# Where one of seven weight sums is made: on GpSimd from loaded tiles, or by accumulating transfers

## The chip, the cores and the metric

The kernel runs on one core of a Trainium2 chip. The metric is the device time of one execution in microseconds (us), the median of several runs. A separate profiled execution gives the trace. The engines are called here as in the profile: PE (TensorE, matrix products), DVE (VectorE), ACT (ScalarE), POOL (GpSimd) and SP (SyncE, which issues most loads).

## What is computed

A trunk of two layers, 256 tokens of width 1024, all in fp32. Each layer has two gated feed-forward blocks (FFN) around a mixer and a cross attention. What matters here is the first FFN of the first layer:

```python
def swiglu(h, w_gate, w_up, w_down):
    return (jax.nn.silu(h @ w_gate) * (h @ w_up)) @ w_down

h = x
for i in range(DEPTH):
    h = h + 0.5 * swiglu(rmsnorm(h, ffn1_norm[i]), ffn1_w_gate[i], ffn1_w_up[i], ffn1_w_down[i])
    ...            # mixer, cross attention
    h = h + 0.5 * swiglu(rmsnorm(h, ffn2_norm[i]), ffn2_w_gate[i], ffn2_w_up[i], ffn2_w_down[i])
```

`w_gate` and `w_up` are 1024 x 2816, `w_down` is 2816 x 1024.

## The kernel before

**Products in two halves.** Every fp32 weight tile is split before PE uses it: ACT writes its rounded copy `whi` (line 224), then DVE writes the rest `wlo` = w - `whi` (line 225, `Gran.split`). Each product is then three products on PE (lines 262 to 264, `mm3`): with `whi`, with `wlo`, and with `whi` against the low half of the activations. A piece of weights that is split at once is a "gran" of 128x1024; PE takes 12 products for a gran of the plain kind, 6 for one of the sets below. The tiles for `whi` and `wlo` rotate through four buffers, so splitting runs a few grans ahead of PE and no further.

**The sets of seven products.** Within an FFN, `ffn_hidden` (line 782) computes the hidden columns in chunks of 512. Some chunks get their gate and up columns together by a scheme with seven products in place of eight (`seven`, line 361). The weights of a set are four tiles of 512 x 512: b11 and b21, the upper and lower half of the up columns, b12 and b22, those of the gate columns. Three further operands are sums, described by the class `Sum` (line 180): x2 = x1 + b22 (with x1 = b11 + b12), x4 = x2 + b21 and x3 = b12 + b22. x1 goes to a tile of its own; x2 and x4 are made in place in x1's tile, x3 in place in b12's tile. The order of the products within a set is b11, x1, x2, b22, x3, b21, x4 (the tuple in line 887), each of two grans; between them `share` puts grans of other products, so that PE always has work.

**Who makes the sums.** x1 and x2 are one DVE addition of 128x2048 each (line 203). x3 and x4 are made by two transfers each: POOL issues them (line 199), and they add 512 KB from HBM onto what lies in the tile. `x2.load()` and `x3.load()` are called after the product with x1, `x4.load()` after the product with x2 (line 389). An engine's instructions run in the order in which they stand in its queue; the waits between engines are semaphores that the framework sets from the tiles read and written.

**The first part.** The first FFN (`norm is first_norm`) has three such sets, for the chunks c = 2, 3 and 4. The other three FFNs have four sets each. The first part's sets lie at about 45 to 82, 85 to 127 and 128 to 165 us of the trace.

Of the kernel before, what the change touches and what calls it, by code (L numbers as in the profile page):

```python
# [12 lines left out]
ALU = mybir.AluOpType  # L13
# [44 lines left out]
def trunk(ctx, tc, a, out):  # L58
    nc = tc.nc
# [15 lines left out]
    def acc(name):  # L75
        return pacc.tile([P, 512], F32, name=name, tag="acc")
# [4 lines left out]
    def work(name, n=512, dt=F32):  # L81

        return wk.tile([P, n], dt, name=name, tag="v", bufs=6) if n <= 256 else wk.tile([P, n], dt, name=name, tag="w")
# [24 lines left out]
    class Pipe:  # L108
# [4 lines left out]
        def after(self, us, f):  # L113
            self.q.append((self.t + us, f))
# [30 lines left out]
    class W:  # L145
# [6 lines left out]
        def load(self, k=None, nk=None):  # L152
            if k is None:
                if self.t is not None:
                    return
                k, nk = 0, self.nk
            if self.t is None:
                t = wp.tile([P, 2048], F32, name="w", tag="w")
                self.t = t[:, :self.nk * self.n].rearrange("p (k c) -> p k c", c=self.n)
            r0 = (self.k0 + k) * P  # L160
            nc.sync.dma_start(self.t[:, k:k + nk, :], self.src[r0:r0 + nk * P, self.c0:self.c0 + self.n]
                              .rearrange("(k p) c -> p k c", p=P))
# [17 lines left out]
    class Sum:  # L180
# [5 lines left out]
        def load(self):  # L186
            if self.t is not None:
                return
            self.l.load()
            if self.into is None:  # L190
                self.r.load()
                self.t = wp.tile([P, 2048], F32, name="w", tag="w").rearrange("p (k c) -> p k c", c=512)
            else:
                self.t = self.l.t
            w = self.r
            if self.into == "dma":
                for k in (0, 2):
                    r0 = (w.k0 + k) * P
                    nc.gpsimd.dma_start(self.t[:, k:k + 2, :], w.src[r0:r0 + 2 * P, w.c0:w.c0 + w.n]  # L199
                                        .rearrange("(k p) c -> p k c", p=P), accum_op=ALU.add)  # L200
            else:
                w.load()
                nc.vector.tensor_tensor(self.t, self.l.t, w.t, op=ALU.add)  # L203

    class Gran:

# [54 lines left out]
    def mm3(o, lh, ll, rh, rl, start, stop, onto=False):  # L261
        nc.tensor.matmul(o, lhsT=lh, rhs=rh, start=start, stop=False, skip_group_check=onto)  # L262
        nc.tensor.matmul(o, lhsT=lh, rhs=rl, start=False, stop=False, skip_group_check=onto)  # L263
        nc.tensor.matmul(o, lhsT=ll, rhs=rh, start=False, stop=stop, skip_group_check=onto)  # L264
# [93 lines left out]

    ONTO = {2: 0, 4: 0, 3: 1, 5: 1, 6: 1}

    def seven(b1, b2, x, mix, after, order=(0, 1, 2, 3, 5, 4, 6), second="dma"):

        b11, b21 = (W(b1[0], k, 4, b1[1], 512) for k in (0, 4))
        b12, b22 = (W(b2[0], k, 4, b2[1], 512) for k in (0, 4))
        x1 = Sum(b11, b12)
        x2 = Sum(x1, b22, second)
        x4 = Sum(x2, b21, "dma")
        x3 = Sum(b12, b22, "dma")
        banks = {}

        def a(t, h):
            return lambda k: tuple(v[:, t * P:(t + 1) * P] for v in pipe.need(x, 4 * h + k))

        def s(i):
            return lambda k: tuple(v[:, k * P:(k + 1) * P] for v in pipe.need(mix, i))
        plan = [(x1, s(0)), (b11, a(0, 0)), (b22, s(1)), (x2, s(2)), (b21, a(0, 1)), (x3, s(3)), (x4, a(1, 1))]
        out = []
        for i in order:
            w, lhs = plan[i]
            for k0 in (0, 2):  # L380
                def step(g, i=i, lhs=lhs, k0=k0):
                    if not k0:
                        banks[i] = banks[ONTO[i]] if i in ONTO else acc("seven")
                    for k in range(k0, k0 + 2):
                        lh, ll = lhs(k)
                        mm3(banks[i], lh, ll, g.hi[:, k - k0, :], g.lo[:, k - k0, :], k == 0 and i < 2, k == 3, onto=i in ONTO)
                        pipe.pe(0.68)
                    if k0:
                        for w in {0: (x2, x3), 3: (x4,)}.get(i, ()):
                            w.load()  # L390
                        after(i, banks)
                out.append((Gran(w.k0 + k0, 2, (w, 0, 512)), step))
        return out

    def share(hosts, s, counts):
        out, hosts = [], list(hosts)
        for i, n in enumerate(counts):
            out += hosts[:n] + s[2 * i:2 * i + 2]
            hosts = hosts[n:]
        return out + hosts  # L400
# [235 lines left out]
    first_norm = nrm = Norm(cols0, mixes=True)  # L636
# [145 lines left out]
    def ffn_hidden(nm, l, norm, fin, tail, extra=None):  # L782
# [31 lines left out]
        def extras(c):  # L814
            for i in (2 * c, 2 * c + 1):
                if extra and i in extra:
                    extra[i]()

        def seven_fin(c):
            us, t = {}, {}  # L820

            def after(i, b):
                v = nc.vector

                def copy():
                    t[i] = work(f"p{i}")
                    nc.scalar.copy(t[i], b[i])

                def c12():
                    us[0] = t[3]  # L830
                    v.tensor_tensor(us[0], b[2], t[3], op=ALU.subtract)
                    nc.scalar.copy(b[2], t[1])
                    nc.scalar.activation(us[0], us[0], AF.Silu, scale=norm.col[:, 0:1])

                def c22():
                    us[1] = t[0]
                    v.tensor_tensor(t[0], t[0], b[5], op=ALU.subtract)
                    nc.scalar.activation(t[0], t[0], AF.Silu, scale=norm.col[:, 1:2])
                    if c == 4:
                        extras(6)  # L840

                def up(r):
                    v.scalar_tensor_tensor(us[r], b[i], norm.col[:, r:r + 1], us[r], op0=ALU.mult, op1=ALU.mult)
                    if r:
                        pipe.after(T["hid"], lambda: turn(c, [us[0], us[1]], 512))
                        extras(c)
                pipe.after(0.7, {0: copy, 1: copy, 3: copy, 2: c12, 5: c22, 4: lambda: up(0), 6: lambda: up(1)}[i])
            return after

        def turn(c, us, n):  # L850
            for i in range(0, n // P, 2):
                tp = v2(small_ps("htp"))
                for j in range(2):
                    for t in range(2):
                        nc.tensor.transpose(tp[:, j, t * P:(t + 1) * P], us[t][:, (i + j) * P:(i + j + 1) * P], ident)  # L855
                hi = v2(slot("hid_hi", F32R))
                lo = v2(slot("hid_lo", F32R))
                nc.scalar.copy(hi, tp)
                nc.vector.tensor_tensor(lo, tp, hi.bitcast(F32), op=ALU.subtract)
                for j in range(2):  # L860
                    hid[4 * c + i + j] = (hi[:, j, :], lo[:, j, :])
        wg, wu = a[nm + "_w_gate"][l], a[nm + "_w_up"][l]
        wide([(wg, 0, 512)], norm, "gate", gate_fin(0), **({} if units else dict(single=True, eng=nc.gpsimd)))
        c = HID // 512
# [19 lines left out]
            n += d0[i:j] + d1[i:j]  # L884
        steps = []
        for c, k in counts.items():
            s = seven((wu, c * 512), (wg, c * 512), norm.x, norm.s, seven_fin(c), (1, 0, 3, 2, 5, 4, 6), "dve")
            steps += share(n[:sum(k)], s, k)
            n = n[sum(k):]
        assert not n  # L890
# [3 lines left out]
    def ffn(nm, l, norm, nxt, extra=None):  # L894
        fin = upd(0.5, nxt)
        ffn_hidden(nm, l, norm, fin, lambda hid, wd: down(wd, 1, [(12, 4), (16, 4)], hid, [], 12, fin), extra)
# [218 lines left out]
    def cross_attention(l, norm, kv, nxt):  # L1115
# [86 lines left out]
        wkv = a["xa_w_kv"][l]  # L1202
        q = [g for c in (2, 0) for g in columns(a["xa_w_q"][l], c * 256, norm, "xq", [q_fin(c), q_fin(c + 1)])]
        weave(share(q, seven((wkv, 1024), (wkv, 1536), kv.x, kv.s, mv_fin()), [2, 1, 1, 2, 1, 1, 0]))
        out_b(a["xa_w_o"][l], KT, ot, upd(1.0, nxt), (4, 0))

# [329 lines left out]
    def last(norm):  # L1536
# [71 lines left out]
        def tail(hid_, wd):  # L1608
            hid.append(hid_)
            gr.extend(Gran(k, 2, (w, 0, 512)) for w in [W(wd, k, 4, 512, 512) for k in (12, 16)] for k in (w.k0, w.k0 + 2))  # L1610
            return [(gr[0], run)]
        ffn_hidden("ffn2", 1, norm, first_half, tail, {12: final_gain})
        units.append((gr[1:], run))

# [72 lines left out]
```

## Time and profile before

| | |
|---|---|
| median of three runs | 1257.75 us (1257.62 to 1258.05) |
| profiled execution, its own time | 1258.38 us |
| its span in the trace | 1256.6 us |
| PE busy | 1247.1 us, 99% |
| DVE busy | 1057.2 us, 84% |
| ACT busy | 873.5 us, 70% |
| POOL busy | 162.5 us, 13% |
| granted PE clock, mean | 0.999 |

The trace lists each instruction with its start and length in us, its engine, its line in the kernel and the tiles it writes and reads. A number in square brackets behind an instruction is the time for which its engine stood idle just before, and what ended that idle time. A line such as `x3` at the end says that three like instructions in a row are shown as one, with their time from the first start to the last end. Instructions on DVE overlap a little: the next one starts some 0.07 us before the end that is listed for the one before.

### The profile page before, as it was taken

What the parts mean: (1) busy time and instruction counts of PE and PEld (TensorE: products, weight loads), DVE (VectorE), ACT (ScalarE), POOL (GpSimd) and SP (SyncE); (2) the same over time, 40 slices, a digit from 0 to 9 for tenths busy, and PEclk for the clock granted to TensorE, in tenths of its full rate; (3) what the DMA queues carried; (4) which work ended last, traced back from release to release, by engine and by line L of the source; (5) the groups of instructions that cost most, each with busy time, mean ns of one, the idle gap of its engine ahead of it and who ended that gap; (6) DMA issues with size and microseconds to landing.
All of it is one profiled execution on the core that took longest, in us unless ns stands there. A gap on an engine that the chain in (4) does not pass through costs nothing.

```text
span 1256.6 us, 18186 instructions
## 1 busy us (share of the span) xinstructions
PE 1247.1 (99%) x6751; PEld 1071.7 (85%) x6751; DVE 1057.2 (84%) x1451; ACT 873.5 (70%) x1388; POOL 162.5 (13%) x139
## 2 busy tenths in 40 slices
PE   9999999999999999999999999999999999999997
PEld 7888888788998888888888889999998898888886
DVE  6998787887787999887998976798898887898886
ACT  6676764686676776767776756777876775877772
POOL 1101102101101111110111000022233100011100
PEclk9999999999999999999999999999999999999999
DMA  9989976445776688987879977665636586489961
GB/s 330 301 255 259 314 256 208 137 165 170 222 214 170 165 252 260 293 246 234 240 198 268 311 247 221 192 193 168 201 134 185 169 246 182 157 251 256 258 190 34
DMA packets 161195, 275.03 MB, mean 219 GB/s; under 512 B 7209, under 2 KB 43730, under 8 KB 161106
## 3 DMA queue, kind: packets, MB, share of 16 engines
q1 hardware_dynamic: 137744, 229.75, 53.4%
q0 software_dynamic: 19744, 38.28, 17.7%
q10 hardware_dynamic: 3618, 5.84, 1.4%
q8 instruction: 53, 0.87, 0.3%
q14 instruction: 36, 0.29, 0.1%
HBM read 271.72 MB, written 2.13 MB: 218 GB/s over the span
## 4 chain that ended last, share of the span: by engine, by line
PE 94%; DMA 2%; DVE 2%; ACT 2%; issue 1%; POOLq 0%; POOL 0%; SPq 0%; ACTq 0%; DVEq 0%
PE out L262 9%; PE out L264 9%; PE out L263 9%; PE seven L263 8%; PE seven L262 8%; PE seven L264 8%; PE htp L855 1%; PE up L263 1%; PE up L264 1%; PE up L262 1%; PE xs L264 1%; PE xs L262 1%; PE xq L263 1%; PE xq L264 1%; PE xs L263 1%; PE xq L262 1%
## 5 line engine op out<-in xcount | busy, mean ns | idle before, releaser
L225 DVE TENSOR_TENSOR wlo<-w,whi 128x1024 fp32r<-128x1024 f32 (+2 forms) x532 | 639.4, 1220 | 134.6 <-ACT whi L224 126.8
L224 ACT CAST whi<-w 128x1024 fp32r<-128x1024 f32 (+2 forms) x534 | 551.0, 1039 | 245.2 <-PE out L264 84.0
L262 PE MATMUL out<-whi,hid_hi 128*128 128x512 f32 x336 | 132.3, 394 | 0.0
L264 PE MATMUL out<-whi,hid_lo 128*128 128x512 f32 x336 | 131.0, 390 | 0.0
L263 PE MATMUL out<-wlo,hid_hi 128*128 128x512 f32 x336 | 130.8, 389 | 0.0
L263 PE MATMUL seven<-wlo,s_hi 128*128 128x512 f32 x272 | 106.0, 390 | 0.6 <-DVE wlo L225 0.6
L262 PE MATMUL seven<-whi,s_hi 128*128 128x512 f32 x272 | 106.2, 390 | 0.0
L264 PE MATMUL seven<-whi,s_lo 128*128 128x512 f32 x272 | 105.9, 389 | 0.0
L199 POOL DMA_DIRECT2D w<-in_ffn_w_up_dram x30 | 36.7, 1268 | 346.6 <-DVE wlo L225 339.5
L203 DVE TENSOR_TENSOR w<-w 128x2048 f32<-128x2048 f32 x32 | 73.2, 2287 | 2.0 <-DMA w<-in_ffn_w_gate_dram 1.5
L264 PEld LDWEIGHTS out<-whi,hid_lo 128*128 128x128 f32 x336 | 63.1, 188 | 13.4
L263 PEld LDWEIGHTS out<-wlo,hid_hi 128*128 128x128 f32 x336 | 63.1, 188 | 12.6
L262 PEld LDWEIGHTS out<-whi,hid_hi 128*128 128x128 f32 x336 | 63.1, 188 | 12.5
L262 PE MATMUL seven<-whi,xh 128*128 128x512 f32 x180 | 70.5, 392 | 0.0
L264 PE MATMUL seven<-whi,xl 128*128 128x512 f32 x180 | 70.1, 389 | 0.0
L263 PE MATMUL seven<-wlo,xh 128*128 128x512 f32 x180 | 70.0, 389 | 0.0
L263 PEld LDWEIGHTS seven<-wlo,s_hi 128*128 128x128 f32 x272 | 51.1, 188 | 11.4 <-DVE wlo L225 1.0
L264 PEld LDWEIGHTS seven<-whi,s_lo 128*128 128x128 f32 x272 | 51.1, 188 | 10.7
L262 PEld LDWEIGHTS seven<-whi,s_hi 128*128 128x128 f32 x272 | 51.1, 188 | 10.4
L199 POOL DMA_DIRECT2D w<-in_ffn_w_gate_dram x30 | 36.9, 1467 | 176.2 <-DVE xst L1146 62.3
L264 PEld LDWEIGHTS seven<-whi,xl 128*128 128x128 f32 x180 | 33.8, 188 | 7.1
L262 PEld LDWEIGHTS seven<-whi,xh 128*128 128x128 f32 x180 | 33.8, 188 | 6.8
(395 smaller groups left out, 3013.7 us busy)
## 6 DMA issues: line engine op xcount, KB each, us to landing
w<-in_ffn_w_up_dram SPq DMA_DIRECT2D x40, 1024.0 KB, 7.8
w<-in_ffn_w_down_dram SPq DMA_DIRECT2D x40, 1024.0 KB, 9.3
w<-in_ffn_w_gate_dram SPq DMA_DIRECT2D x38, 1024.0 KB, 8.9
w<-in_ssd_w_in_dram SPq DMA_DIRECT2D x24, 1024.0 KB, 5.4
w<-in_xa_w_kv_dram SPq DMA_DIRECT2D x16, 1024.0 KB, 6.4
w<-in_ffn_w_gate_dram POOLq DMA_DIRECT2D x30, 512.0 KB, 9.7
w<-in_ffn_w_up_dram POOLq DMA_DIRECT2D x30, 512.0 KB, 7.2
w<-in_da_w_in_dram SPq DMA_DIRECT2D x12, 1024.0 KB, 5.2
```

The lines of the kernel that those rows point to most:

```text
L199: nc.gpsimd.dma_start(self.t[:, k:k + 2, :], w.src[r0:r0 + 2 * P, w.c0:w.c0 + w.n] .rearrange("(k p) c -> p k c", p=P), accum_op=ALU.add)
L203: nc.vector.tensor_tensor(self.t, self.l.t, w.t, op=ALU.add)
L224: nc.scalar.copy(hv, src)
L225: self.eng.tensor_tensor(self.lo[:, :, o:o + n], src, hv.bitcast(F32), op=ALU.subtract)
L262: nc.tensor.matmul(o, lhsT=lh, rhs=rh, start=start, stop=False, skip_group_check=onto)
L263: nc.tensor.matmul(o, lhsT=lh, rhs=rl, start=False, stop=False, skip_group_check=onto)
L264: nc.tensor.matmul(o, lhsT=ll, rhs=rh, start=False, stop=stop, skip_group_check=onto)
L855: nc.tensor.transpose(tp[:, j, t * P:(t + 1) * P], us[t][:, (i + j) * P:(i + j + 1) * P], ident)
```

## The change

For the three sets of the first part, x3 is no longer made by the two accumulating transfers. `seven` gets an argument `third`; where it is `"pool"`, `Sum.load` makes sure that b22 is loaded and lets POOL add it to b12's tile in four steps of 128x512. b22 is loaded anyway for its own product and for x2. All other sums, and the sets of the other FFNs, stay as they were.

```diff
@@ class Sum, load
             else:
                 w.load()
-                nc.vector.tensor_tensor(self.t, self.l.t, w.t, op=ALU.add)
+                if self.into != "pool":
+                    nc.vector.tensor_tensor(self.t, self.l.t, w.t, op=ALU.add)
+                    return
+                for k in range(4):
+                    nc.gpsimd.tensor_tensor(self.t[:, k, :], self.t[:, k, :], w.t[:, k, :], op=ALU.add)
@@ seven
-    def seven(b1, b2, x, mix, after, order=(0, 1, 2, 3, 5, 4, 6), second="dma"):
+    def seven(b1, b2, x, mix, after, order=(0, 1, 2, 3, 5, 4, 6), second="dma", third="dma"):
...
-        x3 = Sum(b12, b22, "dma")
+        x3 = Sum(b12, b22, third)
@@ ffn_hidden
-            s = seven((wu, c * 512), (wg, c * 512), norm.x, norm.s, seven_fin(c), (1, 0, 3, 2, 5, 4, 6), "dve")
+            s = seven((wu, c * 512), (wg, c * 512), norm.x, norm.s, seven_fin(c), (1, 0, 3, 2, 5, 4, 6), "dve",
+                      "pool" if norm is first_norm else "dma")
```

POOL's queue before, for the first two sets. In the first set w_584 is b12's tile, which becomes x3, and w_586 is x1's tile, which becomes x2 and then x4; in the second these are w_882 and w_884.

```order
L199 DMA w_584<-in_ffn1_w_gate_dram 128x2x512 [waits DMAHW1_49,DVE_49]
L199 DMA w_584<-in_ffn1_w_gate_dram 128x2x512
L199 DMA w_586<-in_ffn1_w_up_dram 128x2x512 [waits DMAHW4_49,DMAHW0_49,DMAHW5_49,DVE_49,Pool_49]
L199 DMA w_586<-in_ffn1_w_up_dram 128x2x512 [waits DVE_49]
L199 DMA w_882<-in_ffn1_w_gate_dram 128x2x512 [waits DMAHW1_49,DMAHW2_49,DVE_49,DMAHW3_49,Activation_49,Pool_49]
L199 DMA w_882<-in_ffn1_w_gate_dram 128x2x512
```

The same place in the queue with the change, where w_629 is b22's tile of the first set, and w_884 and w_975 are b12's and b22's of the second.

```order
L207 TENSOR_TENSOR w_584<-w_584,w_629 128x512 [waits DMAHW3_49,DMAHW1_49,DVE_49]
L207 TENSOR_TENSOR w_584<-w_584,w_629 128x512 x3
L199 DMA w_586<-in_ffn1_w_up_dram 128x2x512 [waits DMAHW4_49,DMAHW0_49,DMAHW5_49,DVE_49,Pool_49]
L199 DMA w_586<-in_ffn1_w_up_dram 128x2x512 [waits DVE_49]
L207 TENSOR_TENSOR w_884<-w_884,w_975 128x512 [waits DMAHW1_49,DMAHW2_49,DVE_49,DMAHW3_49,Activation_49,Pool_49]
L207 TENSOR_TENSOR w_884<-w_884,w_975 128x512 x3
```

Each pair of transfers has become four additions in the same place, and the first of them waits in the first set for one more load, that of b22.

DVE's queue with the change, from the sum x1 of the first set (w_586 from w_522, which is b11, and w_584) over the splits of x1's two grans and one other gran to the sum x2 and the splits behind it.

```order
L204 TENSOR_TENSOR w_586<-w_522,w_584 128x2048
L863 TENSOR_TENSOR hid_lo_576<-htp_570,hid_hi_575 128x512
L229 TENSOR_TENSOR wlo_583<-w_586,whi_582 128x1024
L229 TENSOR_TENSOR wlo_597<-w_586,whi_596 128x1024
L229 TENSOR_TENSOR wlo_615<-w_616,whi_614 128x1024
L204 TENSOR_TENSOR w_586<-w_586,w_629 128x2048
L229 TENSOR_TENSOR wlo_628<-w_586,whi_627 128x1024
```

Nothing has moved here: the queues of DVE, PE, ACT and SP hold the same instructions in the same order as before, under line numbers that are one to five higher.

## Rows read from the trace of the kernel before

**Rows 1.** The page's head: span, then each engine's busy time, share, instructions.

```profile
span 1256.6 us, 18186 instructions
...
PE 1247.1 (99%) x6751; PEld 1071.7 (85%) x6751; DVE 1057.2 (84%) x1451; ACT 873.5 (70%) x1388; POOL 162.5 (13%) x139
```

**Rows 2.** Waits of PE: us in total, times, longest.

```profile
PE seven L263 <- DVE wlo L225: 0.6, 1, 0.6
```

**Rows 3.** Timeline of PE, first set: start us, us, instruction, idle time before.

```profile
57.93 0.50 PE L263 MATMUL seven<-wlo,s_hi 128*128 128x512 f32 x1 [0.63 <-DVE wlo L225]
...
68.72 0.39 PE L262 MATMUL seven<-whi,s_hi 128*128 128x512 f32 x1
```

**Rows 4.** Timeline of DVE, first set.

```profile
48.42 0.68 DVE L859 TENSOR_TENSOR hid_lo<-htp,hid_hi 128x512 fp32r<-128x512 f32 x1
49.68 3.60 DVE L225 TENSOR_TENSOR wlo<-w,whi 128x1024 fp32r<-128x1024 f32 x3 [0.58 <-ACT whi L224]
53.20 2.28 DVE L203 TENSOR_TENSOR w<-w 128x2048 f32<-128x2048 f32 x1
56.66 6.90 DVE L225 TENSOR_TENSOR wlo<-w,whi 128x1024 fp32r<-128x1024 f32 x6 [1.17 <-ACT whi L224]
```

**Rows 5.** Busy us of PE, PEld, DVE, ACT, POOL in one stretch, set 2.

```profile
83.40:98.00 14.60, 14.60 (x74) 12.22 (x74) 14.60 (x16) 9.53 (x14) 0.80 (x1) 1.00 0.79 239
```

**Rows 6.** Timeline of POOL, first set and the attention behind it.

```profile
48.82 2.61 POOL L199 DMA_DIRECT2D w<-in_ffn_w_gate_dram  x2 [27.51 <-DVE w L203]
58.42 2.42 POOL L199 DMA_DIRECT2D w<-in_ffn_w_up_dram  x2 [6.99 <-issue]
...
202.36 1.29 POOL L930 TENSOR_TENSOR rt<-rt,rt 128x512 f32<-128x512 f32 x1 [9.90 <-DVE rt L929]
...
244.87 3.53 POOL L930 TENSOR_TENSOR rt<-rt,rt 128x512 f32<-128x512 f32 x2 [12.35 <-DVE rt L929]
```

**Rows 7.** Loads issued at 24 to 29, 69, 110 us: KB, us to landing; SP timeline.

```profile
w<-in_ffn_w_gate_dram SPq DMA_DIRECT2D x2, 1024.0 KB, 15.0
...
69.26 0.37 SPq L161 DMA_DIRECT2D w<-in_ffn_w_gate_dram  x1
w<-in_ffn_w_gate_dram SPq DMA_DIRECT2D x1, 1024.0 KB, 8.3
...
109.80 0.37 SPq L161 DMA_DIRECT2D w<-in_ffn_w_gate_dram  x1
w<-in_ffn_w_gate_dram SPq DMA_DIRECT2D x1, 1024.0 KB, 5.5
```

**Rows 8.** Timeline of DVE: one operation without POOL, three around POOL's adds.

```profile
93.42 1.21 DVE L225 TENSOR_TENSOR wlo<-w,whi 128x1024 fp32r<-128x1024 f32 x1
...
244.28 0.41 DVE L929 TENSOR_TENSOR rt<-k,cossinr 128x256 f32<-128x256 f32 x1
...
245.54 0.41 DVE L929 TENSOR_TENSOR rt<-k,cossinr 128x256 f32<-128x256 f32 x1
...
247.18 2.30 DVE L225 TENSOR_TENSOR wlo<-w,whi 128x1024 fp32r<-128x1024 f32 x1
```

**Rows 9.** Timeline of DVE, second set.

```profile
78.84 0.74 DVE L843 SCALAR_TENSOR_TENSOR p<-seven,rcol,p 128x512 f32<-128x512 f32 x1
...
80.89 2.58 DVE L225 TENSOR_TENSOR wlo<-w,whi 128x1024 fp32r<-128x1024 f32 x2 [0.18 <-ACT whi L224]
```

**Rows 10.** Timeline of PE: first use of two `wlo`, second and third set.

```profile
95.25 0.39 PE L263 MATMUL out<-wlo,hid_hi 128*128 128x512 f32 x1
...
125.16 0.39 PE L263 MATMUL out<-wlo,hid_hi 128*128 128x512 f32 x1
```

**Rows 11.** Timeline of DVE, third set.

```profile
117.27 0.68 DVE L837 TENSOR_TENSOR p<-p,seven 128x512 f32<-128x512 f32 x1
...
119.68 2.36 DVE L225 TENSOR_TENSOR wlo<-w,whi 128x1024 fp32r<-128x1024 f32 x2 [0.59 <-ACT whi L224]
...
122.62 3.48 DVE L225 TENSOR_TENSOR wlo<-w,whi 128x1024 fp32r<-128x1024 f32 x3
```

## The prediction

> **What bounds the kernel now.** I read the page's head first: TensorE (PE) is busy for 1247.1 us of a span of 1256.6 us [rows 1]. So nearly nothing can be won by freeing another engine, and whatever makes PE wait is added to the time in full. The waits of PE come next: apart from its start, the only one of note is 0.6 us, once, in the very stretch that the change touches, and it is a wait for VectorE's (DVE's) subtraction `wlo` [rows 2]. In the order of time this is the product with x2 of the first set: PE stands until 57.93 us, because the low half of the first half of x2 is ready only then [rows 3]. Then I read DVE around it [rows 4]: after the sum x1 come a `hid_lo` at 48.42, three `wlo` from 49.68, the sum x2 at 53.20, and from 56.66 the `wlo` that PE waits for. So in the first set a chain on DVE has no slack at all. In the second set DVE has no idle time either: it is busy for all 14.60 us from 83.40 to 98.00 [rows 5].
>
> The transfers are no bound that PE feels: in this first part no wait of PE leads to one.
>
> **What is removed.** Per set, two accumulating transfers of 512 KB by GpSimd (POOL), whose issue takes 2.61 us of POOL [rows 6], an engine that is idle for most of the time; nobody waits for these transfers in the trace. The other loads may land earlier without them. What that can be worth is bounded by what PE loses today in this stretch, 0.63 us [rows 3]; a loss there is no reason for. I take 0, since the wait of 0.63 us is for DVE and not for a load.
>
> **What is added.** Per set, four adds on POOL of 128x512, both inputs and the output in SBUF. The trace has the same operation elsewhere: 1.29 us alone [rows 6]. Four are 5.16 us. Behind them in the POOL queue are the transfers for x4, which go out at 58.42 in the first set, 9.6 us after the others [rows 6], and wait for splits of x2; even with every add doubled by waiting (10.3 us) they would hardly be held up. The product with x3 starts at 68.72 [rows 3], some 10 us after that, so the wait for x3 itself costs nothing.
>
> **When the adds start.** They wait for the sum x1 (DVE reads b12, which POOL overwrites) and for b22, which must now have landed. In the first set b22 is asked for before 29 us and lands 15.0 us after [rows 7], before the sum x1 ends. So the adds start where the transfers started, released by that sum, at 48.82 [rows 6]. In the second set b22 is asked for at 69.26 and lands after 8.3, at 77.6; in the third at 109.80 and after 5.5, at 115.3 [rows 7].
>
> **What an add costs DVE.** This is the term that decides. At 244.87 two adds stand ready on POOL while DVE has four `wlo` in a row; each `wlo` reads two inputs from SBUF, as the adds do. The two adds take 3.53 us instead of 2.6 [rows 6], and the `wlo` at 247.18 takes 2.30 us instead of the 1.21 of the one at 93.42 [rows 8]. So the two engines take turns: a whole add goes in between two `wlo`, and DVE stands still for 1.09 us. The DVE operation at 245.54, which reads one of its inputs from PSUM, takes 0.41 us during an add, as its like at 244.28 does before it [rows 8]: it isn't touched. The price is thus 1.09 us for each add that meets `wlo` work or a sum, and nothing beside a PSUM operation or an idle DVE. Its bounds are 0 and 1.29, the whole length of an add.
>
> The Trainium skill (SBUF — State Buffer, section "Who interferes with whom") says that a VectorE instruction with two SBUF inputs and a GpSimd instruction that reads SBUF exclude each other for the whole instruction, and that the loser waits outright. It speaks against this change; with the whole 1.29 us in place of the 1.09 us of the row, the sum below would be 9.8 us. The trace agrees that one waits outright, yet shows the smaller 1.09.
>
> **Set 1.** Four adds, 4 x 1.09 = 4.36 us. The first starts at 48.82, beside the `hid_lo` (PSUM) and an idle DVE until 49.68 [rows 4], which covers 0.86. Between 49.68 and the end of the sum x2 there are four DVE operations that all read SBUF twice, so all four adds get their turn before x2 is summed: DVE is 4.36 - 0.86 = 3.5 us late with x2. Nothing is left to take that up: PE already waits for the `wlo` behind it. **PE +3.5 us.**
>
> **Set 2.** The adds come in from about 78.9. Two of them run beside p operations with PSUM, the one at 78.84 and a second like it behind the two `wlo` of 80.89 (0.74 each, of which 0.66 pass before the next start: 1.3 covered), and DVE's small waits for ACT cover 0.4: 0.18 named before 80.89, and 0.22 between these two `wlo`, which take 2.58 [rows 9] where two without a gap take 2.36 [rows 11]. That leaves 4.36 - 1.3 - 0.4 = 2.65 us. Since DVE is then without a gap, it carries this lateness to the `wlo` at 93.42, which would end at 94.6 and which PE needs at 95.25 [rows 8, 10]: 0.6 of slack. **PE +2.0 us.**
>
> **Set 3.** From 115.6. The p operation at 117.27 covers 0.6, an idle 0.59 us before 119.68 the same [rows 11]: 4.36 - 1.2 = 3.15 us. The first `wlo` of the three at 122.62 ends at 123.8 and is needed at 125.16 [rows 10, 11]: 1.3 of slack. **PE +1.8 us.**
>
> After each set DVE has gaps again, so nothing is carried on. PE has no idle time later in which the delay could vanish.
>
> **Sum.** 3.5 + 2.0 + 1.8 = 7.3 us. The profiled execution took 1258.38 us, 1.78 more than its span, and lies 0.63 above the median of the runs, 1257.75; 1258.38 + 7.3 = 1265.7 for it, and 1257.75 + 7.3 = **1265.0 us** as a median.
>
> **The rivals.**
> - *Only the first set pays.* The slack that I read in sets 2 and 3 is of single steps; should b22 land some us later than worked out, or PE's own delay in set 1 leave DVE ahead, the adds would meet idle DVE time. Then 1257.75 + 3.5 = 1261.2. For it: DVE does stand idle before 119.68 [rows 11]; against it: the gapless stretch in set 2 [rows 5]. Chance 0.16.
> - *The whole instruction is lost*, 1.29 us each, whether by turns or in one block of four: 5.16 - 0.86 = 4.3; 5.16 - 1.7 - 0.6 = 2.85; 5.16 - 1.2 - 1.3 = 2.65; together 9.8, 1267.5. With no cover at all it would be 3 x 5.16 = 15.5, 1273.2, which I think out of reach. This is where the page's rule leads. Chance 0.12.
> - *Not slower: DVE goes first.* If DVE, with its next operation ready, is always served before a waiting add, the adds use DVE's gaps alone. In the first set these are 0.86 us from 48.82, 1.17 before 56.66 [rows 4] and the PSUM operations behind; with its product at 68.72, x3 would still be about in time. PE would lose nothing, and at best win back its 0.63 us: 1257.1 to 1259. It decides at the sum x2: if that starts near 53.2, this rival holds. Against it speaks the `wlo` of 2.30 us [rows 8], where an add got its turn although DVE had more work. Chance 0.11 with its near forms.
> - *Faster.* Lighter transfers can give at most the 0.63 us, unless they speed up something that the trace doesn't show. Chance 0.02.
>
> **How the numbers follow.** The forecast, turns at 1.09 us in all three sets, has 0.59 and covers 1262.5 to 1267; the two neighbours add 0.28. The range goes from 1260.5, just below the case of one set, to 1269.5, which takes in the whole instruction lost; what is left out is the rival that isn't slower, faster, and an uncovered loss above. 0.2% is 2.5 us, about what a measurement of this kernel can tell from no change. Slower by more than that: 0.59 + 0.16 + 0.12 = 0.87; within it: 0.11; faster: 0.02.
>
> **What would show it.** In the profile after: four POOL adds from about 48.8 us that last 1.3 to 2.3 each; DVE's `wlo` in 49 to 56 us at 2.3 instead of 1.2; the sum x2 starting at about 56.7 instead of 53.2; a PE wait of some 3.5 to 4 us for `wlo`, partly already at x1; further PE waits of about 2 us near 100 and 130 us (by the shifted clock); and the rest as before. If DVE's `wlo` stay at 1.2 us while POOL's adds are long, or the waits of PE stay below 1 us in all, I am wrong.

## The result

The changed kernel takes 1266.89 us (median of 6 runs, 1266.25 to 1268.08), the kernel before 1257.85 in the same comparison: 9.0 us more, a ratio of 1.0073 (95% interval 1.0060 to 1.0086). The six runs differ in PE's mean granted clock: the three at 0.998 or 0.999 took 1266.25 to 1266.60, the three at 0.997 took 1267.18 to 1268.08. What that means comes out in the experiments. The forecast was 1265.0, with a range of 1260.5 to 1269.5.

The page's head after, beside [rows 1]: DVE is busy for 9.7 us more, POOL for 17.3, and the span is 8.0 us longer: PE is idle for 5.8 us more and busy for 2.2 us more.

```profile
span 1264.6 us, 18182 instructions
...
PE 1249.3 (99%) x6751; PEld 1070.3 (85%) x6751; DVE 1066.9 (84%) x1451; ACT 873.4 (69%) x1388; POOL 179.8 (14%) x145
```

The waits of PE (us in total, times, longest), where [rows 2] had one line of 0.6 us: all new ones end with a split, and none with a load or with x3. They make up the idle time; where the longer busy time of PE comes from isn't broken down here.

```profile
PE out L267 <- DVE wlo L229: 2.5, 2, 2.0
PE seven L266 <- ACT whi L228: 1.6, 1, 1.6
...
PE seven L267 <- DVE wlo L229: 1.3, 2, 0.8
PE gate L267 <- DVE wlo L229: 0.6, 1, 0.6
```

POOL's timeline in the first set (start us, us, instruction, idle time before): the line at 48.31 is the four adds together, the one at 51.81 a single one of them.

```profile
48.31 8.00 POOL L207 TENSOR_TENSOR w<-w 128x512 f32<-128x512 f32 x4 [27.27 <-DVE w L204]
...
51.81 2.27 POOL L207 TENSOR_TENSOR w<-w 128x512 f32<-128x512 f32 x1
```

DVE's timeline beside it; the last line is a single one of the three `wlo`:

```profile
49.40 5.76 DVE L229 TENSOR_TENSOR wlo<-w,whi 128x1024 fp32r<-128x1024 f32 x3 [0.58 <-ACT whi L228]
55.09 3.37 DVE L204 TENSOR_TENSOR w<-w 128x2048 f32<-128x2048 f32 x1
59.63 6.95 DVE L229 TENSOR_TENSOR wlo<-w,whi 128x1024 fp32r<-128x1024 f32 x6 [1.17 <-ACT whi L228]
...
50.61 2.32 DVE L229 TENSOR_TENSOR wlo<-w,whi 128x1024 fp32r<-128x1024 f32 x1
```

Beside [rows 4]: the three `wlo` take 5.76 us instead of 3.60, the sum x2 takes 3.37 instead of 2.28, and a single `wlo` 2.32 instead of 1.21. An add takes 2.27 where it takes 1.29 alone: each engine stands while the other has its turn. PE pays at the next grans, as its timeline has it; the wait for ACT's `whi` at 59.65 is of the same making, since ACT can round x2 only when the late sum is done:

```profile
55.22 0.50 PE L267 MATMUL gate<-wlo,xh 128*128 128x512 f32 x1 [0.57 <-DVE wlo L229]
59.65 0.50 PE L266 MATMUL seven<-whi,s_hi 128*128 128x512 f32 x1 [1.62 <-ACT whi L228]
60.91 0.50 PE L267 MATMUL seven<-wlo,s_hi 128*128 128x512 f32 x1 [0.76 <-DVE wlo L229]
```

How much each set costs is read best from PE's own clock, since PE's order is the same in both kernels: the start of the same product before and after. The places are: ahead of the first set, after its x2, after the delay in the second set, and after the third. PE's timeline of the kernel before:

```profile
42.84 0.39 PE L262 MATMUL gate<-whi,xh 128*128 128x512 f32 x1
...
60.56 0.39 PE L262 MATMUL gate<-whi,xh 128*128 128x512 f32 x1
...
100.46 0.39 PE L262 MATMUL seven<-whi,s_hi 128*128 128x512 f32 x1
...
133.99 0.39 PE L262 MATMUL seven<-whi,s_hi 128*128 128x512 f32 x1
```

PE's timeline of the changed kernel, the same products:

```profile
42.57 0.39 PE L266 MATMUL gate<-whi,xh 128*128 128x512 f32 x1
...
63.57 0.39 PE L266 MATMUL gate<-whi,xh 128*128 128x512 f32 x1
...
106.25 0.39 PE L266 MATMUL seven<-whi,s_hi 128*128 128x512 f32 x1
...
142.41 0.39 PE L266 MATMUL seven<-whi,s_hi 128*128 128x512 f32 x1
```

The differences are -0.27, 3.01, 5.79 and 8.42 us. So the first set costs 3.3 us, the second 2.8, the third 2.6, together 8.7. The span grows by 8.0 only: the earlier start takes back 0.3, and some 0.4 comes back later in the program, at a place that was not established.

### The profile page after: what moved, and what is told of

The parts are those of the page before. It is cut to its first block, busy times and chain, and to the rows that moved or that the text cites. A ratio compares the mean times of both kernels' runs of the same rounds, so it can differ in the third digit from the quotient of the medians.

```text
span 1264.6 us, 18182 instructions
## 1 busy us (share of the span) xinstructions
PE 1249.3 (99%) x6751; PEld 1070.3 (85%) x6751; DVE 1066.9 (84%) x1451; ACT 873.4 (69%) x1388; POOL 179.8 (14%) x145
## 4 chain that ended last, share of the span: by engine, by line
PE 92%; DVE 4%; issue 2%; DMA 1%; ACT 1%; POOLq 0%; POOL 0%; DVEq 0%; ACTq 0%; SPq 0%
PE out L267 9%; PE out L268 9%; PE out L266 9%; PE seven L267 8%; PE seven L266 8%; PE seven L268 8%; DVE wlo L229 2%; PE xs L268 2%; PE xs L266 2%; PE xs L267 2%; PE htp L859 1%; PE up L267 1%; PE mk L266 1%; PE up L268 1%; PE mk L268 1%
## 5 line engine op out<-in xcount | busy, mean ns | idle before, releaser
L229 DVE TENSOR_TENSOR wlo<-w,whi 128x1024 fp32r<-128x1024 f32 (+2 forms) x532 | 647.8, 1236 | 132.3 <-ACT whi L228 124.5
L199 POOL DMA_DIRECT2D w<-in_ffn_w_gate_dram x24 | 29.4, 1464 | 116.7 <-DVE xst L1151 62.5
L267 PEld LDWEIGHTS seven<-wlo,xh 128*128 128x128 f32 x180 | 33.8, 188 | 8.7 <-DVE wlo L229 1.9
```

The costliest lines, as they stand in the source:

```text
L229: self.eng.tensor_tensor(self.lo[:, :, o:o + n], src, hv.bitcast(F32), op=ALU.subtract)
```

## The experiments

All are edits of the changed kernel. "The first set alone" and so on is said of the sets that get POOL adds; the others keep their transfers. The cost of a set is always read as above, from the start of the same products on PE.

**One set at a time.**

```diff
-                      "pool" if norm is first_norm else "dma")
+                      "pool" if norm is first_norm and c == 2 else "dma")
```

(c == 3 and c == 4 for the second and the third.)

> Adds on GpSimd in the first set alone; the other two sets keep their accumulating transfers. Theory (turns: each add takes a DVE turn of 1.09 us, and PE pays what no gap of DVE and no slack covers): the three sets are independent, so the first one costs what PE's clock shows for it in the changed kernel, 3.3 us: 1257.85 + 3.3 = 1261.1 us. Rival (interaction: a part of the 9 us comes from loads and sets that shift against each other): the first set alone costs the same 3.3 us, but the single sets together give less than the whole, about the 7.3 us of the prediction.

> Adds on GpSimd in the second set alone. Theory (turns, sets independent): 2.8 us, 1260.6 us. Rival (interaction): PE comes to this set without the delay of the first and b22 lands where it did before, 1 us later against the DVE work, so that the adds miss one more turn: 2.0 us as predicted, 1259.8 us.

> Adds on GpSimd in the third set alone. Theory (turns, sets independent): 2.6 us, 1260.4 us. Rival (interaction): in the changed kernel DVE's sum x1 of this set waited 0.6 us longer for its load than before, behind transfers for x4 of the second set that came later; with the second set as it was, this goes, and the cost is 1.8 to 2.0 us, 1259.7 to 1259.9 us.

| | median us | ratio to before (95%) | cost in the trace |
|---|---|---|---|
| first set | 1262.55 | 1.0035 (1.0023 to 1.0046) | 4.8 us |
| second set | 1261.01 | 1.0027 (1.0016 to 1.0037) | 3.7 us |
| third set | 1259.46 | 1.0013 (1.0004 to 1.0023) | 1.9 us |

The third comes out where the rival with interaction put it. The first two cost more than either theory had, and their traces show why in a column that had played no part so far: PE's granted clock. The busy times of the first set alone in stretches of 2 us (PE, PEld, DVE, ACT, POOL, then granted clock, DMA share, GB/s):

```profile
60.00:62.00 2.00, 1.24 (x5) 0.86 (x5) 2.00 (x2) 2.00 (x3) 0.43 (x1) 1.00 0.00 0
62.00:64.00 2.00, 2.00 (x6) 1.57 (x5) 2.00 (x3) 1.58 (x2) 2.00 (x2) 0.53 0.20 17
64.00:66.00 2.00, 2.00 (x7) 1.56 (x6) 1.49 (x2) 0.84 (x2) 0.19 (x1) 0.62 1.04 182
66.00:68.00 2.00, 2.00 (x11) 1.62 (x10) 1.23 (x1) 1.22 (x2) 0.00 (x0) 1.00 1.06 321
```

The changed kernel in one of these stretches:

```profile
62.00:64.00 2.00, 2.00 (x10) 1.65 (x9) 2.00 (x2) 1.67 (x3) 2.00 (x2) 1.00 0.31 20
```

After the same pauses (those at 59.65 and 60.91 in the changed kernel), the granted clock falls to 0.5, 1.2 GHz instead of 2.4, for some 3.4 us in one execution, and not at all in the other. PE does 6 products in the 2 us where it did 10. In the second set alone the same happens at 97 us, after a pause of 1.83 us.

**The same two kernels again**, to see whether the fall of the clock goes with the kernel or with the execution.

> The changed kernel again, for its spread and for PE's granted clock. In its first profile the clock stayed at full speed (1.00) through all its pauses, while the first set alone showed 0.5 (1.2 GHz of 2.4) for some 3.4 us after the same pause, and lost about 1.5 us more. Theory (the fall of the clock is a matter of the execution): times of 1266 to 1268 us, and a profile that, where it shows a fall behind a pause, is longer by about 1.5 us for each. Rival (the fall belongs to the kernel with one set): 1.00 throughout again and a spread no wider than that of the kernel before, 0.5 us.

> The first set alone again. Theory (the fall of the clock is a matter of the execution): times fall in two groups, about 1261 us (pauses of PE alone, 3.3 us) and about 1262.5 us (one fall of the clock behind them, 1.5 us more); the profile belongs to the one or the other by its granted clock after 62 us. Rival (a constant cost of 4.7 us): all times at 1262.5.

The changed kernel: 1266.53 us (1266.03 to 1267.08; ratio 1.0069, 1.0054 to 1.0084), again at full clock, with sets of 3.3, 2.8 and 2.5 us on PE's clock. The first set alone: 1261.48 us (1260.60 to 1262.93; 1.0027, 1.0016 to 1.0038), and its profile again shows the fall, from 62 to 66 us, and a cost of 4.9 us. The profiled executions of this kernel took 1262.68 and 1262.93 us, near the upper end; the fastest took 1260.60 and 1260.72. With 3.3 us for the pauses, which it shares with the changed kernel (the same 1.6, 0.8 and 0.6 us of named waits), the fall accounts for 1.5 to 1.6 us, and 1257.9 + 3.3 = 1261.2 lies in the lower part of its times. Two clean groups of times, as the theory had it, do not appear, and both profiles of this kernel show the fall. But each run's mean granted clock sorts them: over both measurements the four runs at 0.999 took 1260.60 to 1261.40 us, the four at 0.997 or less 1262.59 to 1264.82, and the seven at 0.998 lie between, from 1260.64 to 1262.55. (3.4 us at half speed take some 0.0014 off the mean of the whole run, an estimate from the rows above.) The runs of the changed kernel divide in the same way (see the result): three of the first six show the lower clock, none of the four here. As far as the mean clock tells, then, the fall goes with the execution and not with the kernel, as the theory had it; its price is measured, and why it comes in one execution and not in another stays open. Without it the changed kernel costs about 8.5 us; the rest of the 9.0 is the clock in half of the first six runs.

Taking 1.6 us off the first two (the price measured in the first set; for the second it is taken over), the single sets cost 3.2, 2.1 and 1.9 us, 7.2 in all, against 8.7 together: the interaction is real, about 1.5 us, and lies in the second and third sets. Below it says where.

**Nothing in place of the transfers.**

```diff
+            if self.into == "none":
+                return
             w = self.r
...
-                      "pool" if norm is first_norm else "dma")
+                      "none" if norm is first_norm else "dma")
```

> Neither transfers nor adds for x3 in the first part's three sets: b12 stands in for the sum (this leaves the sum out). Theory (turns): the removed transfers were worth nothing to PE, 1257.2 to 1257.9 us, and the wait of PE for x2's wlo (0.63 us) stays. Rival (the transfers slowed the loads): PE's one wait goes too and something hidden with it, below 1257.0 us.

1257.65 us, ratio 1.0000 (0.9991 to 1.0010), with PE's wait for x2's `wlo` still there:

```profile
PE seven L269 <- DVE wlo L231: 0.6, 1, 0.6
```

The three pairs of transfers cost the kernel before nothing that can be measured. Nor can another way to make x3 in the first part, if it changes nothing else, be expected to gain more than the total absence of this work.

**GpSimd writes, but doesn't read.**

```diff
                 for k in range(4):
-                    nc.gpsimd.tensor_tensor(self.t[:, k, :], self.t[:, k, :], w.t[:, k, :], op=ALU.add)
+                    nc.gpsimd.memset(self.t[:, k, :], 0.5)
+                    nc.gpsimd.memset(self.t[:, k, :], 1.0)
```

> In place of each add, two fills of the same 128x512 with a constant on GpSimd: it writes SBUF but reads nothing (this leaves the sum out). Theory (turns taken for SBUF reads): DVE's wlo beside the fills stay at 1.2 us and the time is that of the kernel before, 1257.5 to 1258.2 us. Rival (any GpSimd instruction on SBUF takes DVE's turn): wlo at 1.5 us or more beside the fills, and 1260 us or more.

1257.72 us, ratio 0.9999 (0.9989 to 1.0008). POOL's timeline at the adds' place in the first set:

```profile
47.97 0.99 POOL L207 MEMSET w<- 128x512 f32 x2 [27.25 <-DVE w L204]
48.90 1.00 POOL L208 MEMSET w<- 128x512 f32 x2
49.84 1.00 POOL L207 MEMSET w<- 128x512 f32 x2
50.78 0.99 POOL L208 MEMSET w<- 128x512 f32 x2
```

DVE's timeline beside it:

```profile
49.08 3.62 DVE L230 TENSOR_TENSOR wlo<-w,whi 128x1024 fp32r<-128x1024 f32 x3 [0.58 <-ACT whi L229]
52.61 2.29 DVE L204 TENSOR_TENSOR w<-w 128x2048 f32<-128x2048 f32 x1
```

POOL writes the same tile for 3.8 us, 2.7 of them beside DVE's three `wlo`, and these take 3.62 us, as before the change. What takes DVE's turns is that POOL reads SBUF. That is what the Trainium skill says (SBUF — State Buffer, "Who interferes with whom"): a VectorE instruction with two SBUF inputs contends with a GpSimd instruction that reads SBUF, and not with one that only writes it. This run agrees with 1.2 us per `wlo`, the changed kernel with 2.3.

**Two of the four adds.**

```diff
-                for k in range(4):
+                for k in range(2):
```

> Only two of the four adds in each set (half of x3 is left without its second addend). Theory (turns with covers): the covers stay and the price halves: set 1 pays 2 x 1.09 - 0.86 = 1.3 us, sets 2 and 3, whose covers and slack were 2.4 and 2.5 us, 0 to 0.5 each; together 1.3 to 2.3 us, 1259.2 to 1260.2 us. Rival (a cost in proportion to the adds): half of 9.0, 1262.4 us.

1261.43 us, 1.0027 (1.0017 to 1.0037): 3.4 us more, above the first theory and below the rival; the interval reaches both, so the single sets have to decide. On PE's clock the sets cost 1.1, 0.6 and 1.7 us. The first two are about what the covers leave (expected 1.3 and at most 0.5), where half of the whole would be 1.6 and 1.4; the third is not. There DVE's sum x1 waits for its load for 1.80 us (1.28 before), as in the changed kernel; DVE's timeline:

```profile
114.40 2.29 DVE L204 TENSOR_TENSOR w<-w 128x2048 f32<-128x2048 f32 x1 [1.80 <-DMA w<-in_ffn_w_gate_dram]
116.61 3.45 DVE L229 TENSOR_TENSOR wlo<-w,whi 128x1024 fp32r<-128x1024 f32 x2
```

and the two `wlo` behind it, which take 3.45 us instead of some 2.35 because an add comes in between, are needed by PE early. Half of the adds cost 40% of the whole.

**One add of 128x2048.**

```diff
-                for k in range(4):
-                    nc.gpsimd.tensor_tensor(self.t[:, k, :], self.t[:, k, :], w.t[:, k, :], op=ALU.add)
+                nc.gpsimd.tensor_tensor(self.t, self.t, w.t, op=ALU.add)
```

> One add of 128x2048 in each set instead of four of 128x512. Theory (turns: DVE loses the time for which GpSimd reads, in whatever pieces): one POOL instruction of 4.4 to 5 us, one DVE operation per set longer by up to as much, and about the same total, 1265.5 to 1267.5 us, with a larger single wait of PE at x1. Rival (a fixed price for each turn, whatever its length): one turn per set, 1258 to 1259 us.

1270.78 us, 1.0100 (1.0083 to 1.0117): slower than four steps. DVE loses 3.4 + 4.4 + 4.3 = 12.1 us, against 10.5 with four steps (below), and now at one operation or two. POOL's one add takes 4.60 us in the first set, and DVE's first `wlo` takes 4.58 us, 3.4 more than [rows 8], and the pairs in the second and third set 6.76 and 6.70, where a pair takes 2.36 [rows 11]. POOL's timeline, then DVE's:

```profile
49.15 4.60 POOL L206 TENSOR_TENSOR w<-w 128x2048 f32<-128x2048 f32 x1 [27.82 <-DVE w L204]
```

```profile
50.25 4.58 DVE L228 TENSOR_TENSOR wlo<-w,whi 128x1024 fp32r<-128x1024 f32 x1 [0.58 <-ACT whi L227]
...
80.39 6.76 DVE L228 TENSOR_TENSOR wlo<-w,whi 128x1024 fp32r<-128x1024 f32 x2
...
123.00 6.70 DVE L228 TENSOR_TENSOR wlo<-w,whi 128x1024 fp32r<-128x1024 f32 x2
```

So the price is POOL's reading time and not a price per turn; the rival is out. The expected total is missed by 3 us and more: on PE's clock the sets cost 3.3, 4.0 and 5.1 us, and behind the long pauses of the second and third the granted clock falls, as it did not in the changed kernel's profiles (the same columns as above):

```profile
86.00:88.00 2.00, 0.79 (x3) 0.67 (x4) 2.00 (x3) 0.03 (x1) 0.07 (x1) 1.00 0.00 0
88.00:90.00 2.00, 2.00 (x6) 1.33 (x5) 2.00 (x2) 1.05 (x1) 0.00 (x0) 0.56 0.69 253
...
130.00:132.00 2.00, 2.00 (x5) 1.57 (x6) 1.43 (x2) 1.67 (x3) 0.00 (x0) 0.50 0.37 118
```

With 1.5 us for each of the two, some 9.3 us remain for the pauses, not much above the 8.7 of four steps: most of the difference is the clock.

**The same adds later.** x3 made as x2 - b11 can only start after the sum x2.

```diff
-        x3 = Sum(b12, b22, third)
+        x3 = Sum(b12, (x2, b11), third) if third == "pool" else Sum(b12, b22, third)
...
+            elif self.into == "pool":
+                s, d = w
+                for k in range(4):
+                    nc.gpsimd.tensor_tensor(self.t[:, k, :], s.t[:, k, :], d.t[:, k, :], op=ALU.subtract)
```

> The same four POOL operations per set, but x3 is made as x2 - b11, which can only start once DVE has summed x2. Theory (turns with covers): the adds no longer delay the sum x2, and in set 1 they start at about 55.6 us, the first beside DVE's gap of 1.2 us; three more take turns from the wlo of x2 and what follows, whose slack in the trace of before grows from 0.3 to 2.3 us: PE +1.9 us; sets 2 and 3, where the adds start near 92 and 135 us with PSUM work and gaps close behind, +0.3 and +0.6 us: together 2.8 us, 1260.6 us, with 1260 to 1262.5 allowed for pauses of PE after which its granted clock falls. Rival (twelve adds cost their 9 us wherever they stand): 1266 to 1267 us.

1267.92 us, 1.0080 (1.0065 to 1.0095), a clear miss, yet set by set, read here at products behind the later adds, the working held: 1.8 us in the first set (expected 1.9) and 0.4 in the second (0.3), and at the adds of the third, 0.6 (0.6). The rest, some 7 us, comes from elsewhere, and a fall of the clock is part of it. With b11 read again late, its buffer comes free late: SyncE's queue stands until POOL's last subtraction in the second set is done (waits of SP, 85 to 112 us):

```profile
SPq L161 <- POOL w L204: 15.4, 1, 15.4
```

Two loads of 1024 KB then go out at 101.60 and 102.07 (83.50 and 94.69 in the kernel before), just ahead of x4's transfers at 103.19 and of the load of b12 at 107.49, which itself is only 3.1 us later than before, as PE is. DVE's sum x1 of the third set waits for that load, as its timeline shows:

```profile
121.28 2.29 DVE L208 TENSOR_TENSOR w<-w 128x2048 f32<-128x2048 f32 x1 [6.61 <-DMA w<-in_ffn_w_gate_dram]
```

The edit had changed two things, the time of the adds and the life of a tile. As a test of "where they stand decides" it holds for the first two sets.

**The sum on DVE.** The first attempt left the order to the scheduler, the second holds PE's order.

```diff
-                      "pool" if norm is first_norm else "dma")
+                      "dve" if norm is first_norm else "dma")
...
-        for gs, f in units[2:written[0]]:
+        with tc.manual_schedule(engines={E.PE}):
+            for gs, f in units[2:3]:
+                f(*gs)
+        for gs, f in units[3:written[0]]:
```

(The lines behind the "..." are of the second alone.)

> x3 as one DVE addition of 128x2048, as x2 is made; no POOL adds and no transfers. DVE has to do 2.28 us more per set, half of the 4.36 us that the four POOL adds take from it. Theory (DVE's time is what is lost, less gaps): set 1 pays 2.2 - 1.17 = 1.0 us, since the addition stands right behind the sum x2 where DVE idles for 1.17 us; set 2 nothing, set 3 some 0.3: 1259.1 us, between 1258.5 and 1260.5. Rival (DVE is not what PE waits for, but x3 or the loads): 1257.9 us, or as slow as with POOL, 1266 us.

> x3 as one DVE addition of 128x2048 per set, as in the run with the addition on DVE, but with PE's instructions held in the order of the kernel before (there the scheduler had moved some). Theory (DVE's time is what is lost, less gaps): set 1 pays 2.2 - 1.17 = 1.0 us, set 2 nothing, since the addition stands behind the two wlo that have the least slack, set 3 some 0.3: 1259.3 us, half a microsecond more if the clock falls behind a pause. Rival (what costs is not DVE's time but the making of x3 on the core at all, its wait for b22 and the lost transfers): near 1266 us.

1261.59 us (1.0032, 1.0019 to 1.0045) and 1262.54 us (1.0034, 1.0022 to 1.0047). The first is inconclusive, since the scheduler moved products on PE with it. In the second the first set costs 0.95 us (expected 1.0) and the second nothing, as expected; the third costs 3.5 instead of 0.3, again with a sum x1 that waits for its load, now for 4.43 us. What is shown is that the first set is cheaper with the sum on DVE (0.95) than on POOL (3.3), and that the rival is out for the first two sets: this sum, too, needs b22 and has no transfers, and cost 0.95 us and nothing. The whole, 4.6 us above the kernel before in the second attempt, is half of what the adds on POOL cost, and still no gain.

**The wait for b12's load in the third set** was thus longer in several runs where nothing had been done to it. Ahead of this load POOL issues the transfers for x4 of the second set, which wait for splits of x2. The later these come, the nearer to the load:

| kernel | x4 transfers, us | b12's load, us | apart | DVE's wait for it, us |
|---|---|---|---|---|
| second set alone | 99.51 | 107.90 | 8.39 | none |
| before | 97.20 | 104.36 | 7.16 | 1.28 |
| third set alone | 98.20 | 105.36 | 7.16 | 1.21 |
| nothing in place | 96.64 | 103.79 | 7.15 | 1.41 |
| writes only | 96.64 | 103.77 | 7.13 | 0.86 |
| one add of 128x2048 | 105.26 | 112.22 | 6.96 | 1.46 |
| first set alone | 102.11 | 109.03 | 6.92 | 1.52 |
| first set alone, again | 102.39 | 109.28 | 6.89 | 1.49 |
| two of four adds | 98.96 | 105.50 | 6.54 | 1.80 |
| after | 103.66 | 110.19 | 6.53 | 1.86 |
| after, again | 104.17 | 110.70 | 6.53 | 1.72 |
| on DVE, PE's order moved | 99.66 | 104.61 | 4.95 | 3.78 |
| on DVE, PE's order held | 102.56 | 107.48 | 4.92 | 4.43 |
| later adds | 103.19 | 107.49 | 4.30 | 6.61 |

Over all 14 profiles the wait grows as the two come nearer. At the same distance it still differs by up to 0.65 us (3.78 and 4.43; 0.86 and 1.41), so the single difference of 0.6 us between before and after is no more than such spread and counts only as part of the trend. That the two transfers delay each other is argued from this; no run took it apart, and in the run with later adds other loads stand close by as well.

## Why the prediction was right

**What bounds the kernel** held: every added wait of PE is in the time, and nothing in the rest of the program took more than 0.4 us of it back.

**What an add costs DVE**, 1.09 us by [rows 8], held nearly to the digit: 2.31 to 2.32 us for a `wlo` with an add in between. Over the three sets the 52 `wlo` of the stretch went from 61.9 to 71.3 us and the six sums from 13.7 to 14.8. The group of DVE's `wlo` before, 45 to 142 us (count, busy us, mean ns, idle time before):

```profile
L225 DVE TENSOR_TENSOR wlo<-w,whi 128x1024 fp32r<-128x1024 f32 x52 | 61.9, 1220 | 12.0 <-ACT whi L224 11.4
```

The groups of the `wlo` and of the sums after, 45 to 152 us:

```profile
L229 DVE TENSOR_TENSOR wlo<-w,whi 128x1024 fp32r<-128x1024 f32 x52 | 71.3, 1403 | 9.9 <-ACT whi L228 9.2
L204 DVE TENSOR_TENSOR w<-w 128x2048 f32<-128x2048 f32 x6 | 14.8, 2464 | 1.9 <-DMA w<-in_ffn_w_gate_dram 1.9
```

That is 10.5 us of the 13.1 that twelve adds could take, the rest being cover. The rival with the whole 1.29 us is out, and so is the one in which DVE goes first: the sum x2 starts at 55.09 and takes 3.37.

**What is removed** was worth nothing, as taken (1257.65 without transfers and adds).

**Set 1**: 3.5 forecast, 3.3 measured, twice. The adds start at 48.31, 0.08 us after the sum x1 ends, where the transfers had started 0.31 after it; so the first add is covered by the `hid_lo` and the idle DVE for 1.09 us instead of 0.86, its whole price, and three turns of 1.09 remain. The sum x2 started at 55.09 and not at the 56.7 given as a sign, because the fourth turn fell inside the sum, which took 3.37 us.

**Set 2**: 2.0 forecast, 2.8 measured; alone it is 2.1 without the clock's part. The term that was mis-sized is the cover, which was put too large. I had the first add come in beside the p operation; in the changed kernel it comes earlier, already between the two `wlo` ahead of it (DVE's timeline):

```profile
79.58 3.45 DVE L229 TENSOR_TENSOR wlo<-w,whi 128x1024 fp32r<-128x1024 f32 x2
82.95 0.74 DVE L847 SCALAR_TENSOR_TENSOR p<-seven,rcol,p 128x512 f32<-128x512 f32 x1
83.61 6.13 DVE L229 TENSOR_TENSOR wlo<-w,whi 128x1024 fp32r<-128x1024 f32 x3
...
99.64 4.61 DVE L229 TENSOR_TENSOR wlo<-w,whi 128x1024 fp32r<-128x1024 f32 x4
```

b22 was asked for at 72.27 and landed after 7.0 us instead of the 8.3 of [rows 7], so the adds start at 79.89, and by then DVE, which shares PE's delay, is 3 us behind. In the second set alone the first add is asked for at 77.50, has to wait for the pair, and meets the p operation as forecast. DVE's `wlo` at 99.64 is 6.2 us later than in [rows 8], 3.2 of it from this set (2.65 forecast); less the 0.6 of slack that is 2.6 for PE, and a few tenths went at the grans of b11 before.

**Set 3**: 1.8 forecast, 2.6 measured, 1.9 alone. Here a step was missing: that the delay of the second set moves its x4 transfers nearer to the load that this set's sum x1 waits for. The sum waits 1.86 us for it instead of 1.28; that the nearer transfers are the cause is argued from the table above (DVE's timeline):

```profile
119.20 2.29 DVE L204 TENSOR_TENSOR w<-w 128x2048 f32<-128x2048 f32 x1 [1.86 <-DMA w<-in_ffn_w_gate_dram]
121.41 3.45 DVE L229 TENSOR_TENSOR wlo<-w,whi 128x1024 fp32r<-128x1024 f32 x2
```

I had also taken the slack at one `wlo` only, the first of three; the run with two adds shows that PE feels the lateness earlier, at the pair behind the sum, where two adds alone cost 1.7 us. So does the run with the third set alone: 1.3 of its 1.9 us are lost before the product that I had read (125.16 in [rows 10]), most of it at a product that is 5.4 us ahead of that one in the kernel before (PE's timeline):

```profile
121.65 0.50 PE L267 MATMUL out<-wlo,hid_hi 128*128 128x512 f32 x1 [0.58 <-DVE wlo L229]
```

That 1.8 and 1.9 lie so near is therefore in part luck.

**The sentence that sets carry nothing on** was thus wrong by about 1.5 us, the interaction. The sum, 7.3, stands against 8.7 on PE's clock and 9.0 in the medians, where half of the runs also have a fall of the clock, which the prediction had no term for. The range had room for it through the neighbouring rival, though for another reason than that rival's.

## What to carry to other kernels

Before moving an elementwise operation to an idle GpSimd, look at what VectorE runs beside it: where that reads two inputs from SBUF, GpSimd's reading time is taken out of VectorE's, and four adds that GpSimd does cost VectorE nearly twice what it would need itself (4 x 1.09 against 2.2 us of its time for the same sum). Time such a sum by the chain it stands beside: the same adds cost PE 3.3 us ahead of the sum x2 and 1.8 behind it. And when an edit makes a queue late by 0.6 us, ask what its transfers will meet.

## What the runs showed that was not expected

- **A pause of PE can cost more than its length.** After named pauses of 1.6 and 0.8 us (first set) or 1.8 us (second set) the granted clock was at 0.5 for some 3.4 us, 1.2 GHz in place of 2.4, and PE lost about 1.5 us more; with 4.5 us of pause in the run with later adds it stood there for 6.8 us. The changed kernel, with the same pauses in its first set, showed it in neither of two profiles, but three of its ten runs have the lower mean clock and the longer time that go with it. What decides is open.
- **One long read was worse than four short ones**, 12.8 against 9.0 us: DVE loses 12.1 us instead of 10.5, single waits of PE are longer, and in its profile the clock falls behind two of them. Without these falls the two would be about 9.3 and 8.7 us.
- **Writes of POOL are free for DVE here**: 2.7 us of fills beside `wlo` that keep their usual 1.2 us.
